# Recurrence levels on TensorE taken two at a time, with copies of half of q, in a two-layer hybrid model on one core

## The chip, the cores and the metric

The kernel runs on one core of a Trainium2 chip, in float32. The metric is the device time of one execution in microseconds, the median of several runs. [...] Each engine runs its own list of instructions in order and waits on semaphores for the others.

## What is computed

Two layers over a sequence of 256 tokens and 1024 features. Each layer is: feed-forward, a mixer, cross-attention over 256 memory rows, feed-forward, each with a residual and a layer norm. The change is inside the mixer, in the gated linear recurrence (four heads, 128 by 128 state). From the reference, cut:

```python
f = lb + (1.0 - lb) * jax.nn.sigmoid(f_logit)      # decay, per token and feature
k = 1.0 - f
def step(state, inp):                              # one chunk of tokens
    b = jnp.cumsum(lb_, axis=2)                    # lb_: log f
    decay = exp(b[t] - b[s]) for s <= t, else 0
    attn = einsum('bhtd,bhsd,bhtsd->bhts', qb, kb, decay)
    o = attn @ vb + (qb * exp(b)) @ state
    ...
o = o * rsqrt(mean(o**2) + RMS_EPS) * norm_g * sigmoid(g)
```

Beside the recurrence the mixer has a gated short convolution and a pooling over windows of 2, 4, 8 and 16 tokens; the three results are joined and multiplied by `w_out`.

## The kernel before, in words

All large products are made with weights split in a high and a low half: ScalarE casts the high half (`whi`, L61), VectorE subtracts to get the low half (`wlo`, L62), and TensorE adds three products (hi x hi, hi x lo, lo x hi; `product`, L105). Raw weights come by SP's DMAs into six buffers (`raw`, L77); a buffer is free for the next load when both halves have been made from it. There are eight buffers each for `whi` and `wlo`.

`mixer` (L779) makes, from one weight matrix `w_in`, the decay `f` and `k = 1 - f`, then `q`, and after that, piece by piece, the values `v` (in four half-products), the pooling input `pu` (two), the convolution's `cv` (four) and `u` (two). These twelve pieces are a generator, `between` (L855); `products_of_others(n)` (L863) takes the next n of them. So the big products are spread between the steps of the recurrence, on TensorE in the order in which the code is written (`manual_schedule`, L867). On the other engines a scheduler orders the instructions, except in the short VectorE part at L1008.

The recurrence isn't computed token by token. The decay between two tokens is a product of `f` over the tokens between them, and it is built over seven levels of block size c = 1, 2, 4, ..., 64 (`LEVELS`). At level c, tokens in the later block of each pair of blocks attend to those in the earlier block. `k` and `q` carry the decay up to the edge of their block:

- `q` is first multiplied by `f` in place (L892); before that, the squares (L888) multiply `k` and `q` of the same block of 32 tokens, and the diagonal is kept by a mask (L889).
- `blocks(c)` (L896) copies the earlier blocks of `k` to a dense tile `kc` on ScalarE (L899), with two buffers.
- At L923, 16 matmuls of 128x32 weights (four groups of PSUM partitions by four heads) multiply `kc` and the later blocks of `q`, which are read in place with a stride.
- VectorE then multiplies half of `k` (L935) and half of `q` (L938) by the block products `tot`, in place, for the next level. The product with `q` has to wait until TensorE has read `q` at this level.
- What a level gives is kept from PSUM: below 32 by a masked copy into `square` (L947), from 32 on by ScalarE into `AT` (L960); `square` itself goes to `AT` at L957.

In the profile each of these float32 matmuls appears as two records: the squares as 64, a level as 32. Between two levels stand one or two pieces of the other products.

After the last level come the product of the first half's `k` with the second half's `q` (L971, copied to `AX_`, L972), the recurrence's two products with `v` (L981, L982), its norm (`ss`: squares on ScalarE L986, a power on POOL L988), and the gate's four products. `yr` (L995) is dealt by small DMAs (L1002) and transposed back (L1058). The pooling sums go through two tiles `pw` in turn (L1024, L1030), end in `win` (L1032) and are multiplied on TensorE (L1047), between the gate's last product and the four products for the attention's keys (`fill`, L1061). `project_back` then multiplies by `w_out` in slabs of two row blocks, in the order 0, 6, 2, 4.

Of the kernel before, what the change touches and what calls it, by code (L numbers as in the profile page):

```python
# [8 lines left out]
F32 = mybir.dt.float32  # L9
# [3 lines left out]
ALU = mybir.AluOpType  # L13
# [4 lines left out]
P = 128  # L18
DEPTH = 2
SEQ = 256  # L20
DM = 1024
DFF = 2816
NT = SEQ // P
NK = DM // P
HEADS = 4
# [4 lines left out]
LEVELS = (1, 2, 4, 8, 16, 32, 64)  # L30
WINDOWS = (2, 4, 8, 16)
PAD = 16
# [14 lines left out]
def model(ctx: ExitStack, tc: tile.TileContext, t: dict, out: bass.AP):  # L47
    nc = tc.nc
# [5 lines left out]
    def acc(shape=(P, 2, SEQ), tag="acc"):  # L54
        return ps.tile(list(shape), F32, tag=tag, name=tag)
# [88 lines left out]
    h = [cst.tile([P, DM], F32, name=f"h{i}") for i in range(NT)]  # L144
# [69 lines left out]
    idc = consts[:, 0:32]  # L214
# [564 lines left out]
    def mixer(l, fill):  # L779
        w_in = t["w_in"][l]  # L780
        with tc.tile_pool(name="mix", bufs=1, reuse_waits="tile") as mp:
# [81 lines left out]
            def products_of_others(n):  # L863
                for _ in range(n):
                    next(fill_in)
# [18 lines left out]
            o = acc((P, NT, HEADS, 32), "dn")  # L884
            for b in range(NT):
                for hh in range(HEADS):
                    for g in groups:
                        nc.tensor.matmul(o[g, b, hh, :], k[:, b, hh, g], q[:, b, hh, g], start=True, stop=True)  # L888
            nc.vector.tensor_tensor(  # L889
                square, o, idc[:, None, None, :].to_broadcast([P, NT, HEADS, 32]), op=ALU.mult  # L890
            )
            nc.vector.tensor_tensor(q, q, f, op=ALU.mult)  # L892
            qf, kf = q[:, :, :, :], k[:, :, :, :]
            tot = f.rearrange("p b h s -> p (b h s)")

            def blocks(c):  # L896

                kc = mp.tile([P, HEADS, P], F32, tag="kc", name="kc", bufs=2)
                nc.scalar.copy(  # L899
                    kc.rearrange("p h (a w c) -> p w (h a) c", w=2, c=c),  # L900
                    view(kf, 0, (other + c, 2), (2 * c, HEADS * 64 // c), (1, c), keep=True),
                )
                return kc

            def later(j, c):

                at = (j * 32 // c ^ 1) * c
                return slice(at, at + c)

            kc = blocks(1)  # L910
            for n, c in enumerate(LEVELS):
                a = 64 // c
                products_of_others((1, 2, 1, 2, 1, 2, 2)[n])


                o = acc((P, HEADS, max(c, 32)), "dn")
                for hh in range(HEADS):
                    for j, g in enumerate(groups):
                        if c < 32:
                            x = view(qf, hh * P + 32 * j + c, (other - c, 2), (2 * c, 16 // c), (1, c))  # L920
                        else:
                            x = q[:, j * 32 // c % 2, hh, later(j, c)]
                        nc.tensor.matmul(o[g, hh, :], kc[:, hh, g], x, start=True, stop=True)  # L923
                na, tb = HEADS * a, other // c
                q2 = view(qf, c, (other - c, 2), (2 * c, na), (1, c))
                k2 = view(kf, 0, (other + c, 2), (2 * c, na), (1, c))
                tq = bass.AP(
                    tensor=tot.tensor, offset=tot.offset,
                    ap=[list(tot.ap[0]), [tb + 1, 2], [2, na]] + ([[0, c]] if c > 1 else []),
                )  # L930
# [4 lines left out]
                nc.vector.tensor_tensor(k2, k2, tk, op=ALU.mult)  # L935
                if c < 64:
                    kc = blocks(2 * c)
                nc.vector.tensor_tensor(q2, q2, tq, op=ALU.mult)  # L938
                if c < 64:
                    nt = mp.tile([P, NT * na], F32, name=f"tot{c}")  # L940
                    t2 = tot.rearrange("p (a w) -> p a w", w=2)
                    nc.vector.tensor_tensor(nt, t2[:, :, 0], t2[:, :, 1], op=ALU.mult)
                    tot = nt[:, :]
                if c < 32:
                    o = o.rearrange("p h (b t) -> p h b t", b=NT)
                    for b in range(NT):
                        nc.vector.copy_predicated(  # L947
                            square[:, b].rearrange("p h (a w c) -> p h a w c", w=2, c=c)[:, :, :, 1 - b, :],
                            masks[:, b, n, :].rearrange("p (a c) -> p a c", c=c)[:, None].to_broadcast(
                                [P, HEADS, 16 // c, c]  # L950
                            ),
                            o[:, :, b].rearrange("p h (a c) -> p h a c", c=c),
                        )
                else:
                    if c == 32:
                        for g in groups:
                            nc.scalar.copy(AT[g, :, :, g], square[g])  # L957
                    for at in range(0, P, c):
                        g = slice(at, at + c)
                        nc.scalar.copy(AT[g, at // c % 2, :, later(at // 32, c)], o[g])  # L960
            w_gate = load(w_in, 0, NK, 2304, 512)

            def gate(j, o=None):
# [257 lines left out]
```

## Time and profile before

| | before |
|---|---|
| median of 3 runs | 1070.83 us (1070.54 to 1071.65) |
| span of the profiled execution | 1068.8 us |
| mean granted TensorE clock | 0.998 |
| VectorE, ScalarE busy | 946.3 us, 642.4 us |
| one mixer's recurrence, first layer | 212.5 to 255.3 us from the span's start |
| the same, second layer | 738.8 to 781.6 us |

The span goes from the first to the last instruction of one profiled execution; it has no time of its own beside the span, and the runs' median is 2.0 us longer. In a row of the timeline the numbers are the start, how long the group took, the engine, the line and operation, out <- in, the shape and the count; a note in brackets tells of idle time before it and what ended it. PE is TensorE's matmul, PEld its weight load. L numbers are lines of the kernel above.

### The profile page before, as it was taken

Reading aid. Unit: us, or ns where it says so; the run is one execution under the profiler, and the core shown is the slowest. Engines: PE = TensorE matmul, PEld = TensorE weight load, DVE = VectorE, ACT = ScalarE, POOL = GpSimd, SP = SyncE. Lnnn points to the kernel's source line nnn. Section 1 sums busy time; section 2 is a strip of 40 time slices with the busy share of each in tenths; the row PEclk is TensorE's granted clock in tenths of the full one; section 3 lists DMA queues with packets and bytes.
Section 4 is the critical chain, followed back from the end, with each engine's and each line's share of the span. In section 5 each row is a group of like instructions: output and inputs, shape, how many; then the busy total and the mean of one; then the engine's idle time right before and its main releaser. Section 6 shows DMA issues by size and latency. Waiting matters only on the chain.

```text
span 1068.8 us, 16312 instructions
## 1 busy us (share of the span) xinstructions
PE 1059.3 (99%) x5966; PEld 937.7 (88%) x5966; DVE 946.3 (89%) x1318; ACT 642.4 (60%) x916; POOL 66.4 (6%) x114
## 2 busy tenths in 40 slices
PE   9999999999999999999999999999999999999997
PEld 7888888889899888888888888888898998888886
DVE  6977997998988799999799999788989787999996
ACT  7555664666557565656575557566764665656660
POOL 9700001000000000000000000010000000000000
PEclk9999999999999999999999999999999999999999
DMA  9997484755574575848675865856536665759461
GB/s 362 262 307 256 129 288 165 249 176 174 170 278 167 178 252 194 290 167 218 238 272 184 256 254 183 290 179 216 196 126 213 241 227 181 257 156 334 134 223 40
DMA packets 130895, 231.90 MB, mean 217 GB/s; under 512 B 9408, under 2 KB 48608, under 8 KB 130816
## 3 DMA queue, kind: packets, MB, share of 16 engines
q1 hardware_dynamic: 129024, 228.49, 64.8%
q0 software_dynamic: 1216, 1.20, 0.5%
q8 instruction: 47, 0.77, 0.3%
q10 hardware_dynamic: 576, 1.18, 0.3%
q14 instruction: 32, 0.26, 0.1%
HBM read 216.15 MB, written 1.05 MB: 203 GB/s over the span
## 4 chain that ended last, share of the span: by engine, by line
PE 99%; DMA 0%; DVE 0%; issue 0%; DVEq 0%
PE acc L105 65%; PE dn L105 31%; PE acc L172 1%; PE dn L923 1%; PE dn L982 0%; DMA h<-in_x_dram 0%; PE acc L491 0%; PE dn L981 0%; PE dn L971 0%; PE acc L1047 0%; PE dn L888 0%; DVE h L358 0%; DVE h L353 0%; PE dn L472 0%; DVE st L338 0%
## 5 line engine op out<-in xcount | busy, mean ns | idle before, releaser
L61 ACT CAST whi<-raw 128x1024 fp32r<-128x1024 f32 (+1 forms) x438 | 442.9, 1042 | 197.5 <-DVE raw L597 54.9
L62 DVE TENSOR_TENSOR wlo<-raw,whi 128x1024 fp32r<-128x1024 f32 (+1 forms) x438 | 515.7, 1209 | 32.6 <-ACT whi L61 29.0
L105 PE MATMUL acc<-whi,xT 128*128 128x512 f32 x1032 | 312.9, 380 | 0.0
L105 PEld LDWEIGHTS acc<-whi,xT 128*128 128x128 f32 x1032 | 195.1, 189 | 27.5
L105 PE MATMUL acc<-wlo,xT 128*128 128x512 f32 x516 | 195.6, 379 | 0.0
L105 PE MATMUL acc<-xT,whi 128*128 128x512 f32 x576 | 142.3, 383 | 0.2
L105 PE MATMUL dn<-whi,ah 128*128 128x512 f32 x346 | 131.5, 380 | 0.0
L105 PE MATMUL dn<-wlo,ah 128*128 128x512 f32 x346 | 131.2, 379 | 0.0
L105 PE MATMUL dn<-whi,al 128*128 128x512 f32 x346 | 131.2, 379 | 0.0
L105 PEld LDWEIGHTS acc<-xT,whi 128*128 128x128 f32 x576 | 104.0, 190 | 12.5 <-ACT whi L61 0.7
L105 PEld LDWEIGHTS acc<-wlo,xT 128*128 128x128 f32 x516 | 97.5, 189 | 13.8
L105 PE MATMUL dn<-whi,xT 128*128 128x512 f32 x288 | 87.9, 381 | 0.0
L105 PEld LDWEIGHTS acc<-xT,wlo 128*128 128x128 f32 x576 | 75.5, 191 | 3.9
L105 PE MATMUL acc<-xT,wlo 128*128 128x256 f32 x576 | 75.9, 275 | 0.0
L105 PEld LDWEIGHTS dn<-whi,al 128*128 128x128 f32 x346 | 65.4, 189 | 9.2
L105 PEld LDWEIGHTS dn<-wlo,ah 128*128 128x128 f32 x346 | 65.4, 189 | 9.2
L105 PEld LDWEIGHTS dn<-whi,ah 128*128 128x128 f32 x346 | 65.4, 189 | 9.1
L350 POOL TENSOR_TENSOR rs<-rs,nhalf 128x1 f32<-128x1 f32 x16 | 14.9, 930 | 833.6 <-DVE rs L346 598.1
L597 DVE TENSOR_TENSOR raw<-raw 128x1024 f32<-128x1024 f32 x56 | 66.2, 1217 | 0.4
L105 PEld LDWEIGHTS dn<-whi,xT 128*128 128x128 f32 x288 | 54.4, 189 | 7.7 <-DVE xT L62 0.3
L105 PE MATMUL dn<-wlo,xT 128*128 128x512 f32 x144 | 54.6, 379 | 0.0
L332 DVE SCALAR_TENSOR_TENSOR h<-h,dn 128x512 f32<-128x512 f32 x31 | 21.2, 683 | 32.9 <-PE dn L105 32.9
(234 smaller groups left out, 1277.5 us busy)
## 6 DMA issues: line engine op xcount, KB each, us to landing
raw<-in_ffn_up_dram SPq DMA_DIRECT2D x88, 512.0 KB, 5.3
raw<-in_ffn_down_dram SPq DMA_DIRECT2D x88, 512.0 KB, 6.6
raw<-in_ffn_gate_dram SPq DMA_DIRECT2D x84, 512.0 KB, 5.1
raw<-in_w_in_dram SPq DMA_DIRECT2D x48, 512.0 KB, 4.7
dealt<-sg SPq DMA_DIRECT2D x80, 128.0 KB, 4.7
raw<-in_ca_k_dram SPq DMA_DIRECT2D x16, 512.0 KB, 4.9
raw<-in_w_out_dram SPq DMA_DIRECT2D x16, 512.0 KB, 4.5
raw<-in_ca_v_dram SPq DMA_DIRECT2D x16, 512.0 KB, 5.3
```

The lines of the kernel that those rows point to most:

```text
L61: nc.scalar.copy(hi, src)
L62: lows.append(nc.vector.tensor_tensor(lo, src, hi.bitcast(F32), op=ALU.subtract))
L105: nc.tensor.matmul(o, w, x, start=start, stop=stop)
L172: nc.tensor.transpose(pt[:, k, :], src[:, (4 * j + k) * P : (4 * j + k + 1) * P], unit)
L332: nc.vector.scalar_tensor_tensor(v, v, ALPHA / scale, sums(y[i][n]), op0=ALU.mult, op1=ALU.add, accum_out=None if junk is None else st[:, ...
L350: nc.gpsimd.tensor_tensor(rs, rs, nhalf[:, 0:1], op=ALU.pow)
L597: nc.vector.tensor_tensor(r[i], r[i], plus[i], op=ALU.add)
L923: nc.tensor.matmul(o[g, hh, :], kc[:, hh, g], x, start=True, stop=True)
```

## The change

- Order on TensorE: the squares and level 1 stand directly behind one another, then levels 2 and 4, 8 and 16, 32 and 64, with three pieces of the other products ahead of each of the last three pairs. Before, each level had one or two pieces ahead of it.
- `q * f` goes to a new tile `q1` (the squares still read `q`), and the levels work on `q1`.
- For levels 2, 8 and 32, ScalarE copies the later halves of `q1` to a dense tile `qc`, and the matmuls of that level read `qc`. VectorE's product with `q1` at these levels waits for that copy in place of the level's matmuls.
- `kc` is made for both levels of a pair ahead of it (the same two buffers).
- `qc` and `AX_` no longer have tiles of their own: `qc` lives in the first `pw` tile's place and `AX_` in the second's. The `pw` tiles are made, and their pads cleared by POOL, after the recurrence.

```diff
-            AX_ = mp.tile([P, HEADS, P], F32, name="AX_")
...
-            pw = [mp.tile([P, 2, PAD + SEQ], F32, name=f"pw{n}") for n in range(2)]
-            for x in (pu, *pw):
-                nc.gpsimd.memset(x[:, :, 0:PAD], 0.0)
+            nc.gpsimd.memset(pu[:, :, 0:PAD], 0.0)
+
+            def window(n, name):
+                return mp.tile([P, 2, PAD + SEQ], F32, tag=f"pw{n}", name=name)
+
+            def in_window(n, name):
+                return window(n, name).rearrange("p a t -> p (a t)")[:, 0:512]
...
-            nc.vector.tensor_tensor(q, q, f, op=ALU.mult)
-            qf, kf = q[:, :, :, :], k[:, :, :, :]
+            q1 = mp.tile([P, NT, HEADS, P], F32, name="q1")
+            nc.vector.tensor_tensor(q1, q, f, op=ALU.mult)
+            qf, kf = q1[:, :, :, :], k[:, :, :, :]
...
-            def blocks(c):
+            def earlier_of_k(c):
...
+            def later_of_q(c):
+
+                qc = in_window(0, "qc").rearrange("p (b t) -> p b t", b=NT)
+                nc.scalar.copy(
+                    qc.rearrange("p b (a c) -> p b a c", c=c),
+                    view(qf, c, (other - c, 2), (2 * c, HEADS * 64 // c), (1, c), keep=True),
+                )
+                return qc
...
-            kc = blocks(1)
-            for n, c in enumerate(LEVELS):
-                a = 64 // c
-                products_of_others((1, 2, 1, 2, 1, 2, 2)[n])
...
+            kc = earlier_of_k(1)
+            products_of_others(1)
+            o = acc((P, NT, HEADS, 32), "dn")
+            for b in range(NT):
+                for hh in range(HEADS):
+                    for g in groups:
+                        nc.tensor.matmul(o[g, b, hh, :], k[:, b, hh, g], q[:, b, hh, g], start=True, stop=True)
+            o1 = attention_within(1, kc)
+            of_k(1)
+            kc = earlier_of_k(2)
+            nc.vector.tensor_tensor(
+                square, o, idc[:, None, None, :].to_broadcast([P, NT, HEADS, 32]), op=ALU.mult
+            )
+            of_q(1)
+            kept(0, 1, o1)
+            for n, c in ((1, 2), (3, 8), (5, 32)):
+                qc = later_of_q(c)
+                of_k(c)
+                kd = earlier_of_k(2 * c)
+                of_q(c)
+                products_of_others(3)
+                o = attention_within(c, kc, qc)
+                o2 = attention_within(2 * c, kd)
+                of_k(2 * c)
+                if c < 32:
+                    kc = earlier_of_k(4 * c)
+                of_q(2 * c)
+                kept(n, c, o)
+                kept(n + 1, 2 * c, o2)
+                if c == 8:
+                    for g in groups:
+                        nc.scalar.copy(AT[g, :, :, g], square[g])
+            products_of_others(1)
...
-                nc.tensor.matmul(o[:, hh, :], k[:, 0, hh, :], q[:, 1, hh, :], start=True, stop=True)
+                nc.tensor.matmul(o[:, hh, :], k[:, 0, hh, :], q1[:, 1, hh, :], start=True, stop=True)
+            AX_ = in_window(1, "AX_").rearrange("p (h t) -> p h t", h=HEADS)
             nc.scalar.copy(AX_, o)
...
+            pw = [window(n, f"pw{n}") for n in range(2)]
+            for x in pw:
+                nc.gpsimd.memset(x[:, :, 0:PAD], 0.0)
```

The functions `of_k`, `of_q`, `attention_within` and `kept` hold what the loop over the levels held: the product of half of `k`, the product of half of `q` with the next `tot`, the 16 matmuls, and what keeps a level's result. `attention_within(c, kc, qc)` reads `qc` where one is given and `q1` otherwise.

More of the change, by code (lines that the diff above doesn't have):

```diff
@@ L883, in mixer @@
             groups = [slice(32 * j, 32 * j + 32) for j in range(4)]
[L884 to L891, printed above, removed]
-            nc.vector.tensor_tensor(q, q, f, op=ALU.mult)
-            qf, kf = q[:, :, :, :], k[:, :, :, :]
-            tot = f.rearrange("p b h s -> p (b h s)")
-            def blocks(c):
+            q1 = mp.tile([P, NT, HEADS, P], F32, name="q1")
+            nc.vector.tensor_tensor(q1, q, f, op=ALU.mult)
+            qf, kf = q1[:, :, :, :], k[:, :, :, :]
+            tots = [f.rearrange("p b h s -> p (b h s)")]
+            def earlier_of_k(c):
                 kc = mp.tile([P, HEADS, P], F32, tag="kc", name="kc", bufs=2)
@@ L908, in later, with of_k @@
                 return slice(at, at + c)
-            kc = blocks(1)
-            for n, c in enumerate(LEVELS):
+            def of_k(c):
                 a = 64 // c
-                products_of_others((1, 2, 1, 2, 1, 2, 2)[n])
[L916 to L923, printed above, removed]
                 na, tb = HEADS * a, other // c
-                q2 = view(qf, c, (other - c, 2), (2 * c, na), (1, c))
+                tot = tots[-1]
                 k2 = view(kf, 0, (other + c, 2), (2 * c, na), (1, c))
[L927 to L930, printed above, removed]
                 tk = bass.AP(
@@ L935, in mixer, with of_q @@
                 nc.vector.tensor_tensor(k2, k2, tk, op=ALU.mult)
-                if c < 64:
-                    kc = blocks(2 * c)
+            def of_q(c):
+                a = 64 // c
+                na, tb = HEADS * a, other // c
+                tot = tots[-1]
+                q2 = view(qf, c, (other - c, 2), (2 * c, na), (1, c))
+                tq = bass.AP(
+                    tensor=tot.tensor, offset=tot.offset,
+                    ap=[list(tot.ap[0]), [tb + 1, 2], [2, na]] + ([[0, c]] if c > 1 else []),
+                )
                 nc.vector.tensor_tensor(q2, q2, tq, op=ALU.mult)
@@ L942, in mixer, with attention_within, kept @@
                     nc.vector.tensor_tensor(nt, t2[:, :, 0], t2[:, :, 1], op=ALU.mult)
-                    tot = nt[:, :]
+                    tots.append(nt[:, :])
+            def attention_within(c, kc, qc=None):
+                o = acc((P, HEADS, max(c, 32)), "dn")
+                for hh in range(HEADS):
+                    for j, g in enumerate(groups):
+                        if c < 32:
+                            if qc is None:
+                                x = view(qf, hh * P + 32 * j + c, (other - c, 2), (2 * c, 16 // c), (1, c))
+                            else:
+                                x = qc[:, :, hh * 64 + j * 16 : hh * 64 + j * 16 + 16]
+                        elif qc is None:
+                            x = q1[:, j * 32 // c % 2, hh, later(j, c)]
+                        else:
+                            x = qc[:, j % 2, hh * 64 + j // 2 * 32 : hh * 64 + j // 2 * 32 + 32]
+                        nc.tensor.matmul(o[g, hh, :], kc[:, hh, g], x, start=True, stop=True)
+                return o
+            def kept(n, c, o):
                 if c < 32:
```

6 lines of the change are left out of this document (3 added, 3 removed).

## The prediction

> **What bounds the kernel now.** I read the page first (busy times and the chain that ended last), then who waited for whom on TensorE, then the chain in order of time around one mixer, then the timeline of single instructions there. Two lines of the page, and TensorE's whole list of waits:
>
> ```profile
> span 1068.8 us, 16312 instructions
> PE 1059.3 (99%) x5966; PEld 937.7 (88%) x5966; DVE 946.3 (89%) x1318; ACT 642.4 (60%) x916; POOL 66.4 (6%) x114
> ```
>
> ```profile
> PE dn L472 <- DVE kTh L467: 1.5, 1, 1.5
> PE acc L491 <- DMA h<-in_x_dram: 0.5, 1, 0.5
> ```
>
> TensorE is busy for 99% of the span and waited twice, both at the very start. No other engine is on the path for more than the edges, so time can be won only by giving TensorE less to do, and is lost only by making it wait. VectorE, at 89%, is the engine that could make it wait.
>
> The recurrence of a mixer puts eight short runs of 128x32 matmuls between long runs of 128x128 ones. The timeline shows what each of them costs beyond its own matmuls:
>
> ```profile
> 212.14 0.38 PE L105 MATMUL acc<-whi,xT 128*128 128x512 f32 x1
> 212.45 0.76 PE L888 MATMUL dn<-q,k 128*32 128x32 f32 x64
> 213.47 0.38 PE L105 MATMUL acc<-wlo,xT 128*128 128x512 f32 x1
> ```
>
> ```profile
> 224.59 0.38 PE L105 MATMUL acc<-xT,whi 128*128 128x512 f32 x1
> 224.91 0.46 PE L923 MATMUL dn<-q,kc 128*32 128x32 f32 x32
> 225.29 1.78 PE L105 MATMUL acc<-xT,whi 128*128 128x512 f32 x7
> 226.91 1.05 PE L105 MATMUL acc<-xT,wlo 128*128 128x256 f32 x8
> 227.80 1.89 PE L105 MATMUL acc<-xT,whi 128*128 128x512 f32 x8
> 229.53 1.05 PE L105 MATMUL acc<-xT,wlo 128*128 128x256 f32 x8
> ...
> 233.94 0.46 PE L923 MATMUL dn<-q,kc 128*32 128x32 f32 x32
> ...
> 245.59 0.66 PE L923 MATMUL dn<-q,kc 128*32 128x64 f32 x32
> ```
>
> Undisturbed, eight 512-column matmuls go from start to start in 229.53 - 227.80 = 1.73 us, 0.216 each. Around the level at 224.91 the same eight (one before it, seven behind) take 226.91 - 224.59 = 2.32 us. So a run of 32 small records costs 0.59 us. The run of the squares, L888, has 64 records: 213.47 - 212.14 = 1.33 us for two large matmuls that need 0.43, so it costs 0.90. Twice the records cost 0.31 more, not 0.59 more: **0.28 us of every run is the price of breaking into the large matmuls and returning to them**, and 0.31 is the work. The rows show it on both sides: 0.32 us from the last large matmul's start to the first small one, where 0.22 is usual, and seven large ones in 1.62 us behind it, where 1.51 is usual.
>
> **The change, part by part.**
>
> *Fewer runs on TensorE.* In the order of the changed program as built, the squares and level 1 stand in one run of 96 records, then 2 with 4, 8 with 16 and 32 with 64: four runs per mixer in place of eight. No matmul is added, dropped or resized. Four breaks less in each of two mixers: 8 x 0.28 = 2.24 us. The merged runs aren't in the trace; L888 is the nearest row to them. From both sides: if records in the middle of a run go at the 0.27 us for 32 that the first ones of a run take (0.59 less 0.32), a break is worth 0.32 and the sum 2.5; the lower end follows.
>
> *A wait inside a run.* Level 1, 4, 16 and 64 now follow another small run at once and wait for two engines each; the first wait is an instruction of its own in the queue.
>
> ```profile
> L923 PEld LDWEIGHTS dn<-q,kc x448: 105/113/117, 215.9 to 772.3; 128*32 128x32 f32 x150
> L923 PEldq EVENT_SEMAPHORE  x14: 51/51/51, 215.6 to 769.2; - x14
> ```
>
> ```profile
> 216.00 0.39 PE dn L923 x31
> ...
> 239.83 0.39 PE dn L923 x32
> ...
> 771.96 0.58 PE dn L923 x32
> ```
>
> It takes 51 ns. In the kernel before it ran while large matmuls were still busy: the last one starts at 769.2 and its run at 771.96, a lead of 2.7 us. Inside a run of small records (0.31 us for 32) the lead is shorter, and no row shows such a wait there. Bounds: 0 if the queue still holds 51 ns of work, 8 x 51 ns = 0.41 us if it doesn't. I take 0, since the runs with it (L923) begin as soon after the last large matmul as L888, which has none (0.32 and 0.31 us), and keep 0.41 for the range: the sum is then -1.83. [...]
>
> *The moving operand.* Levels 2, 8 and 32 read q from a dense copy. In the chain's rows above, level 1 with its stride of two (216.00) and level 32, dense already (239.83), both have 0.39 us, so I take nothing, and nothing to lose.
>
> *Three more copies on ScalarE, per mixer.* They have the form of L899 (first row):
>
> ```profile
> L899 ACT COPY kc<-k 128x512 f32<-128x512 f32 x14 | 9.6, 683 | 13.3 <-DVE k L935 11.2 <-DVE k L810 2.1
> L935 DVE TENSOR_TENSOR k<-k,tot 128x512 f32<-128x512 f32 x12 | 8.6, 717 | 1.9 <-ACT kc L899 1.9
> ```
>
> ```profile
> 218.70 2.94 ACT L61 CAST whi<-raw 128x1024 fp32r<-128x1024 f32 x3
> ```
>
> 3 x 0.68 = 2.0 us on an engine that is busy for 60%. They lie in the chain k product (the last row), copy, q copy, q product (0.7 like the k product) that must end before a pair. I walked the new order with these durations and, from start to start, 0.95 us for a cast of weights on ScalarE (three in 2.94) and 1.14 for VectorE's half (four in 4.63, a row below). The pairs' last input is ready at 220.1, 229.2 and 237.5; TensorE reaches them at 224.0, 232.8 and 241.5 (the old starts 224.91, 233.94, 245.59, less the runs, breaks and the one product that no longer stand ahead). Some 4 us are spare at each. The first run is closer: scaled q is ready at 214.0, and its level comes at 215.7. If this cover went, each us late would cost one us.
>
> *q's new home* is the same multiplication into another tile: no cost. It is moved ahead of the squares, which then wait for TensorE alone.
>
> *The window sums go late.* `pw` now shares its two homes with the copy of q and with `AX_`. So `pw1` can be written only after the recurrence's second product, and POOL's clearing of its pad stands behind the first `ss` power. VectorE's busy time by stretch, and what is late next:
>
> ```profile
> 212.00:232.00 20.00, 20.00 (x283) 16.82 (x282) 19.00 (x32) 11.53 (x18) 0.00 (x0) 1.00 0.68 228
> 232.00:249.00 17.00, 17.00 (x191) 15.02 (x190) 15.65 (x35) 12.52 (x25) 0.00 (x0) 1.00 0.51 166
> 249.00:259.70 10.70, 10.70 (x77) 10.09 (x76) 6.58 (x20) 6.63 (x23) 2.03 (x2) 1.00 0.35 115
> 259.70:278.90 19.20, 19.20 (x109) 17.33 (x108) 19.20 (x29) 13.63 (x21) 0.00 (x0) 1.00 0.49 160
> ```
>
> ```profile
> L1024 DVE TENSOR_TENSOR pw<-pw x6: 409/426/677, 231.2 to 760.9; 128x256 f32<-128x256 f32 x4, 128x512 f32<-128x512 f32 x2
> L1024 DVE TENSOR_TENSOR pw<-pu x2: 693/693/693, 229.4 to 755.8; 128x512 f32<-128x512 f32 x2
> ```
>
> ```profile
> 237.10 0.69 DVE L1032 TENSOR_TENSOR win<-win,pu 128x512 f32<-128x512 f32 x1
> ```
>
> ```profile
> L986 ACT ACTIVATE square<-dn 128x128 f32<-128x128 f32 x16 | 4.4, 277 | 1.5 <-PE dn L982 1.1
> ```
>
> ```profile
> 276.60 4.63 DVE L62 TENSOR_TENSOR wlo<-raw,whi 128x1024 fp32r<-128x1024 f32 x4
> ```
>
> ```profile
> 254.87 0.39 PE L982 MATMUL dn<-v,AT 128*128 128x128 f32 x2
> 260.33 1.03 PE L1047 MATMUL acc<-win,wpool 128*128 128x256 f32 x4
> 280.31 0.38 PE L105 MATMUL dn<-wlo,xT 128*128 128x512 f32 x1
> ```
>
> In the stretches the third busy figure is VectorE's: full at 259.7 to 278.9, with 10.70 - 6.58 = 4.1 us free just before. A mixer's window steps (four passes, four small pieces, the subtraction) are 0.69 + 0.68 + 2 x 0.42 + 0.69 + 4 x 0.17 = 3.6 us by their durations and 2.9 in a row, where neighbours overlap by 0.08 as the weight halves do. In the new order only the first pass and piece come before 249; 2.2 us fall into that free time.
>
> The walk: the second product ends at 254.87 + 0.39 - 1.12 = 254.1. Then VectorE does `pw1`, the gate's scaling, the first `yr` and a piece (0.6, 0.5, 0.6 and 0.1: 255.9); `ss` waits for ScalarE's four squares (0.4 each with the read of the sum) and a window pass between them, 256.2; two passes, two pieces, ScalarE's last pass and the subtraction follow (0.3, 0.1, 0.3, 0.1, 0.5, 0.6): 258.2. TensorE asks for `win` at 260.33 - 1.12 = 259.2: 1.0 us spare, where 22 were (237.8 to 260.33). From 258.2 on VectorE has a gate's adds and the second `yr`, 1.0 us, which stood just ahead of 259.7, and then the work of the full stretch, 19.2 us, in another order (one half of w_out's weights now behind the transposes): w_out's last half is made at 278.4. Before, as the second of the four at 276.60, it was made at 278.9. TensorE's first use was at 280.31 and is now at 279.2: 0.8 us spare. SP issues the last w_out load when the late half frees its buffer, near 269 in place of 262; 4.5 us to landing (the median of w_out's loads, below) and a cast end well before VectorE's turn. I cost all this at nothing, with the 1.0 and 0.8 us as the cover that a longer walk would use up. POOL's queue: its next work, the second `ss` power, comes 2 us later than the clearing, so nothing is held.
>
> ```profile
> raw<-in_w_out_dram SPq DMA_DIRECT2D x16, 512.0 KB, 4.5
> ```
>
> **Sum.** -2.24 us on the path of the span of 1068.8 us, which becomes 1066.6. The median of the runs is 1070.83; 2.0 us lie around the span, and nothing in them is touched. Forecast: 1068.6 us, 0.21% less. A difference of 0.2%, 2.1 us, is about what a measurement of this kernel can tell from no change, so the forecast lies at that line.
>
> **The rivals.**
>
> *The wait inside the run shows* (-1.83 us, and down to -1.4 where each pause costs twice its length): 1069.0 to 1069.4, no difference. For it: records follow each other every 8 to 10 ns there. Against it: the lead of 2.7 us.
>
> *The late window work is partly in TensorE's way.* Where VectorE is 0.8 to 2.7 us later than walked, w_out's last half makes TensorE wait by what exceeds 0.8, in each mixer: 1068.6 + 2 x (0 to 1.9), so up to 1072.4. The stretch at 259.7 is full, and my walk has some 30 steps; but the free 4.1 us ahead of it are real.
>
> *Slower: the window work isn't absorbed.* VectorE's free time at 249 to 259.7 is waiting in order for ScalarE and TensorE. If the 2.2 us of window steps don't fit into it and the pass that waits for the second product holds back gate and `yr` by another us, the full stretch ends 3.2 us later than walked. TensorE then waits 3.2 - 0.8 = 2.4 us per mixer against 1.12 saved: +2.6 us, 1073.4. It decides from 3.0 us of lateness on (2 x (3.0 - 0.8 - 1.12) = 2.1). For it: w_out's halves are the only weights without a stretch of spare time ahead of them. Against it: of the 4.1 us, 2 are left by my walk.
>
> *It doesn't do what it says*: the order as built has the four runs, so this could only be a break that stays inside a run, which is the first rival.
>
> **How the numbers follow.** The forecast (-1.9 to -2.6) gets 0.60, five in six of it beyond 0.2%; the exposed wait 0.12; the partial stall 0.11, nearly all within 0.2% either way; the slower case 0.17. Faster 0.50, same 0.10 + 0.12 + 0.11 = 0.33, slower 0.17. The range goes from 1067.9 (-2.5 us and 0.4 for the runs' spread) to 1071.0, which takes in the exposed wait and the smaller stalls and leaves out the slower case and little more.
>
> **What would show it.** In the profile after: four runs per mixer in the chain, of about 96, 64, 64 and 64 records, the large blocks around them with 0.2 us over their undisturbed time once per run; a pair of 32s at 0.9 us in all. A pair near 0.95 to 1.0 is the exposed wait. A row that TensorE waited for VectorE at the pooling product or at w_out's last half is the late window work; its size is the loss. A wait of a pair's first level for ScalarE would mean that the copies lie on the path, which I exclude by 4 us.

## The result, and the profile after

The changed kernel takes 1068.80 us (median of 21 runs, 1068.28 to 1070.98) against 1070.83 for the kernel before (21 runs, 1070.44 to 1071.71): a ratio of 0.9981, 95% interval 0.9975 to 0.9987. That is 2.03 us less, where 2.2 were forecast. The profiled execution has a span of 1067.8 us where 1068.8 stood before, only 1.0 less; experiment 5 takes up the difference.

The page of the kernel after, and TensorE's waits (us in total, times, longest). In these rows DVE is VectorE, ACT is ScalarE, POOL is GpSimd, and SP is SyncE, whose queue issues all 396 loads of `raw`:

```profile
PE 1057.5 (99%) x5966; PEld 938.0 (88%) x5966; DVE 946.6 (89%) x1318; ACT 646.6 (61%) x922; POOL 66.9 (6%) x114
```

```profile
PE dn L472 <- DVE kTh L467: 1.5, 1, 1.5
PE acc L105 <- DVE wlo L62: 0.8, 1, 0.8
PE acc L491 <- DMA h<-in_x_dram: 0.5, 1, 0.5
```

TensorE has the same 5966 records and is busy for 1.8 us less. The second row is new. Its place is 600 us, in a feed-forward block and far from the mixer.

The timeline of the kernel after shows the runs of the first mixer:

```profile
214.80 0.38 PE L105 MATMUL acc<-whi,xT 128*128 128x512 f32 x1
215.11 0.76 PE L980 MATMUL dn<-q,k 128*32 128x32 f32 x64
215.86 0.46 PE L955 MATMUL dn<-q,kc 128*32 128x32 f32 x32
...
216.56 0.38 PE L105 MATMUL acc<-wlo,xT 128*128 128x512 f32 x1
...
223.93 0.38 PE L105 MATMUL acc<-xT,whi 128*128 128x512 f32 x1
224.24 0.46 PE L955 MATMUL dn<-qc,kc 128*32 128x32 f32 x32
224.52 0.49 PE L955 MATMUL dn<-q,kc 128*32 128x32 f32 x32
224.94 1.78 PE L105 MATMUL acc<-xT,whi 128*128 128x512 f32 x7
226.55 1.05 PE L105 MATMUL acc<-xT,wlo 128*128 128x256 f32 x8
```

There are four runs per mixer, as the program says. From the last large start ahead of the pair to the first start of eight behind it go 226.55 - 223.93 = 2.62 us; eight undisturbed ones need 1.73, so the pair costs 0.89 us. That is the price of the 64 records of the squares before (0.90), and 0.28 less than two single levels (2 x 0.59). The first run costs 216.56 - 214.80 - 0.43 = 1.33 us.

Counted run by run in the trace, the small runs cost 5.20 us per mixer before (0.89 + 6 x 0.59 + 0.78). After, they cost 1.33 + 0.89 + 0.89 + 1.08 = 4.19 in the first mixer and 4.08 in the second, whose first run took 1.22. Together that is 2.13 us less.

The late work on VectorE, and where TensorE first needs it (timeline of the kernel after):

```profile
258.00 0.69 DVE L1082 TENSOR_TENSOR win<-win,pu 128x512 f32<-128x512 f32 x1 [0.26 <-ACT win L1080]
...
259.40 1.03 PE L1097 MATMUL acc<-win,wpool 128*128 128x256 f32 x4
...
276.69 4.66 DVE L62 TENSOR_TENSOR wlo<-raw,whi 128x1024 fp32r<-128x1024 f32 x4
...
279.38 0.38 PE L105 MATMUL dn<-wlo,xT 128*128 128x512 f32 x1
```

`win` ends at 258.7 (before the change at 237.8) and is needed at 259.4: 0.7 us spare. The second of the four halves ends at 276.69 + 4.66 / 2 = 279.0 and is needed at 279.38: 0.4 us spare. TensorE waits at neither.

### The profile page after: what moved, and what is told of

It reads as the page before. It is cut to its first block, busy times and chain, and to the rows that moved or that the text cites. A ratio compares the mean times of both kernels' runs of the same rounds, so it can differ in the third digit from the quotient of the medians.

```text
span 1067.8 us, 16332 instructions
## 1 busy us (share of the span) xinstructions
PE 1057.5 (99%) x5966; PEld 938.0 (88%) x5966; DVE 946.6 (89%) x1318; ACT 646.6 (61%) x922; POOL 66.9 (6%) x114
## 3 DMA queue, kind: packets, MB, share of 16 engines
q10 hardware_dynamic: 576, 1.18, 0.3%
## 4 chain that ended last, share of the span: by engine, by line
PE 92%; DVE 5%; issue 1%; DMA 1%; ACT 1%; SPq 0%; DVEq 0%; ACTq 0%
PE acc L105 60%; PE dn L105 30%; DVE wlo L62 2%; PE acc L172 1%; DVE raw L597 1%; DMA dealt<-sg 1%; PE dn L955 0%; ACT whi L61 0%; DMA h<-in_x_dram 0%; PE dn L1029 0%; DVE h L358 0%; DVE sg L440 0%; PE acc L491 0%; DVE square L453 0%; DVE h L353 0%
```

## The experiments

**1. The breaks alone: eight_runs and by_heads.** eight_runs keeps every edit but puts the large products back between the levels:

```diff
-                products_of_others(3)
+                products_of_others(2)
                 o = attention_within(c, kc, qc)
+                products_of_others(2 if c == 32 else 1)
                 o2 = attention_within(2 * c, kd)
```

and the same between the squares and level 1.

> The changed kernel with its eight runs of small matmuls apart again, with large products between them as before the change; q1, the copies of q, the shared homes and the late window sums stay. Theory (a break costs 0.28 us and nothing else of the change has a price): eight breaks more, +2.24 us, 1071.0, the time of the kernel before (1070.8). Rival (the rest of the change gains or costs by itself): the time then lies off the time of the kernel before by that amount, say 1071.5 or more if the late window sums cost, and 1070.3 or less if the copies gain. Rival (the fewer breaks are not the cause): it stays at 1068.8.

Measured: 1070.99 us (11 runs), ratio 0.9999 (0.9990 to 1.0008). So the merged runs are the whole gain. Scaled `q`'s new tile, the copies and the late window sums have together no price that can be measured; in the trace each mixer takes as long as before, within 0.01 us.

by_heads goes the other way. Between the large matmuls of one product, each pair is issued in eight pieces:

```diff
+                for hh in range(HEADS):
+                    pieces.append(lambda hh=hh: attention_within(c, kc, qc, o, [hh]))
+                for hh in range(HEADS):
+                    pieces.append(lambda hh=hh: attention_within(2 * c, kd, None, o2, [hh]))
+                products_of_others(1)
```

> The changed kernel, but each pair's 64 records are issued as eight pieces of 8 records (one head each), one piece behind each of the first large matmuls of the product that stood ahead of the pair. Same matmuls, 7 breaks more per pair, 42 in all. Theory (each break has a fixed price of 0.28 us, however short the run): +11.8 us, 1080.6. Rival (the price is one of filling and emptying a queue, which a piece of 8 records with one large matmul around it doesn't pay in full): half of it or less, +5.9 us, 1074.7. Rival (a piece also loses the overlap of its own records): above 1081.

Measured: 1082.29 us (4 runs), 13.5 more than the changed kernel, or 0.32 per break where the theory had 0.28. Its timeline:

```profile
222.36 0.27 PE L962 MATMUL dn<-qc,kc 128*32 128x32 f32 x8
222.56 0.48 PE L105 MATMUL acc<-xT,whi 128*128 128x512 f32 x1
222.97 0.27 PE L962 MATMUL dn<-qc,kc 128*32 128x32 f32 x8
```

One period, 222.97 - 222.36 = 0.61 us, holds one large matmul (0.216) and eight records (0.08). What is left, 0.31 to 0.32, is the break, and the period repeats as long as large matmuls of 512 columns stand between. The time lies in the range of the second rival (above 1081), but not for its reason: the eight records of a piece start within 0.073 us, as the first eight of a whole run do. So the price doesn't fall with the length of the run, and it is 0.32 rather than 0.28. Merging two runs of 32 wins only 0.28, because the second 32 records of a run go a little slower: start to start the first 32 take 0.27 us and the next 0.30 (trace of the changed kernel, pair at 224.24).

**2. What a break is made of: whole_array.** The levels below 64 use the whole array, without another shape. Only one of four groups of 32 rows of each product is kept, so this version leaves the levels' results out:

```diff
-                        nc.tensor.matmul(o[g, hh, :], kc[:, hh, g], x, start=True, stop=True)
+                        if whole:
+                            nc.tensor.matmul(wide[:, j, hh, :], kc[:, hh, :], x, start=True, stop=True)
...
```

> The changed kernel, but levels 1 to 32 use the whole array: 128x128 weights (a head's whole kc) and the same 32 moving columns, as many matmuls as before, and of the products only one of four groups of 32 rows is kept, so the levels' results are left out. The squares and level 64 keep their 128x32 shape. Theory (the price of a break is that of changing the array's shape): the runs of levels 2 with 4 and 8 with 16 show no gap at their ends, 0.22 us or less from the last large matmul to the first small one and 0.22 from the first large one behind to the next, where the changed kernel has 0.31 and 0.32. Rival (the price is that of going from long to short matmuls): 0.31 and 0.32 stay. The records themselves get longer: the whole-array matmuls of 128 columns start every 0.112 us, a quarter of that is 0.028 per record in place of 0.009, so 12 levels x 32 x 0.019 = +7.3 us, less about 1.2 for four breaks by the theory: 1075; more if short records have a floor above 0.028.

Measured: 1130.19 us (4 runs), far over the 1075. In its timeline are the entry of a whole-array run in the first mixer, the exit of one in the second, and there the step from whole-array records (L961) to those of level 64, which keep the 128x32 shape (L963):

```profile
230.60 0.38 PE L105 MATMUL acc<-xT,whi 128*128 128x512 f32 x1
230.82 1.42 PE L961 MATMUL dn<-qc,kc 128*128 128x32 f32 x12
...
776.05 1.06 PE L961 MATMUL dn<-q,kc 128*128 128x32 f32 x8
776.94 0.46 PE L105 MATMUL acc<-whi,xT 128*128 128x512 f32 x1
777.24 0.38 PE L105 MATMUL acc<-wlo,xT 128*128 128x512 f32 x1
...
827.97 0.39 PE L961 MATMUL dn<-qc,kc 128*128 128x32 f32 x2
828.29 0.26 PE L963 MATMUL dn<-q,kc 128*32 128x64 f32 x4
```

At the entry the usual 0.22 us stand where a 128x32 run has 0.31. At the exit the first large start comes 0.112 us behind the last small one, a record's own length, where a 128x32 run has 0.126 against 0.009 per record; then 0.30 to the next, where it has 0.32. So the 0.09 at the entry goes with the change of shape. The step into level 64 shows it a second time, with short records on both sides: 828.29 comes 0.205 us behind the last L961 start (828.08), 0.09 more than the 0.112 between such records.

The 0.12 at the exit can't be given to the shape by these rows. The whole-array records of this run come 0.112 us behind one another, and where the squares go over into whole-array records of level 1, the first comes 0.125 behind. So by these rows the change of shape adds some 0.01 to the exit, and the rest may be the 0.112 that lie between whole-array records in any case; no run separates the two. Of the last 0.10, 0.08 stays without a change of shape (0.30 where 0.22 is usual). What TensorE does in the 0.09 us at the entry, no row here shows.

The expected time was wrong because a record on the whole array takes 0.112 us with 32 columns (L961 here) as with 128 (L971 of the kernel before), not 0.028. What sets that pace isn't shown: the weight-load records of this run last 186 to 192 ns at the full clock, longer than the 0.112 us from one record to the next, and overlap. Then the granted clock fell as well (stretch of the long run, and a part of it; PEclk is the third figure from the end):

```profile
230.00:241.00 11.00, 11.00 (x75) 10.79 (x75) 3.67 (x9) 1.74 (x4) 0.00 (x0) 0.76 0.37 136
236.00:239.00 3.00, 3.00 (x16) 3.00 (x16) 0.00 (x0) 0.00 (x0) 0.00 (x0) 0.50 0.00 0
```

The 0.76 is a mean: the clock stood at 1.00 and then at 0.50. In the pairs of levels 2 to 16 the fall came between the 34th and the 45th record, after 3.6 to 4.8 us of them, and from there one took 0.213 us. Small tiles are worth their break here.

**3. The cover of the late window work: late_more, late_second, early_windows.** late_more makes the first window pass four times (`for _ in range(1 if g else 4)`), late_second the second pass five times. early_windows gives the sums tiles of their own again:

```diff
-                qc = in_window(0, "qc").rearrange("p (b t) -> p b t", b=NT)
+                qc = q[:, 0].rearrange("p h s -> p (h s)").rearrange("p (b t) -> p b t", b=NT)
...
-            AX_ = in_window(1, "AX_").rearrange("p (h t) -> p h t", h=HEADS)
+            AX_ = mp.tile([P, HEADS, P], F32, tag="kc", name="AX_", bufs=2)
```

> The changed kernel with the first pass of the window sums made four times over (the same sums into the same tile): three passes more on VectorE per mixer, 3 x 0.61 to 0.69 = 1.8 to 2.1 us, in the late place. Theory (VectorE has about 0.4 us to spare at the last half of w_out's weights and 0.7 at the subtraction that ends win): TensorE waits 1.4 to 1.7 us per mixer, +2.8 to +3.4 us, 1071.6 to 1072.2. Rival (VectorE's waits in this stretch take it in): 0 to +0.8 us, 1068.8 to 1069.6, with no wait of TensorE at either place.

> The changed kernel with the second pass of the window sums, the first that has to wait for the recurrence's second product, made five times over: four passes more on VectorE per mixer, 4 x 0.61 = 2.44 us, all of it in the late place. Theory (VectorE has 0.7 us to spare at win, 0.4 at w_out's last half and some 0.5 of waiting in order on the way): TensorE waits some 1.2 us for win and 0.3 more for w_out's last half in each mixer, +3.0 us, 1071.8, between 1071.0 and 1072.9 (nothing taken in on the way). Rival (the stretch takes it in, as it took in most of the three passes made earlier): under 1069.6 and no wait at win.

> The changed kernel with tiles of their own for the window sums again, so that they may run as early as before the change; the copies of q's halves go into q's tile, which is free behind the squares, and AX_ into one of kc's two homes. Runs of small matmuls as in the changed kernel. Theory (the late sums cost nothing): 1068.8, within 0.4 us. Rival (they hold TensorE up for a few tenths in some executions): 1068.0 to 1068.4 and no first use of w_out's last half close behind VectorE.

late_more: 1069.78 us (11 runs; 0.9978 to 0.9996 of before), 1.0 over the changed kernel, where 2.8 to 3.4 had been expected. The first pass needs only `pu`: in the first mixer all four were made by 249.4 us, ahead of the late place, and VectorE was only some 0.35 us late by the end (its last four halves start at 277.03 in place of 276.69, while TensorE was 0.2 us ahead of its place in the changed kernel). The timeline of late_more shows that as a wait, 0.67 us where 0.43 are usual for two:

```profile
278.76 0.59 PE L105 MATMUL dn<-whi,xT 128*128 128x512 f32 x2
279.43 0.48 PE L105 MATMUL dn<-wlo,xT 128*128 128x512 f32 x1
```

So the cover at w_out's last half is some 0.3 us. Each mixer of this profile won 0.74 to 0.77 us where the changed kernel's win 1.13 to 1.15 (experiment 5); that is 0.75 of the 1.0. late_second: 1076.07 us (5 runs), 7.3 over the changed kernel for 2 x 2.44 us of work. TensorE's waits there:

```profile
PE dn L105 <- DVE wlo L62: 3.4, 2, 1.7
...
PE dn L105 <- DVE xT L62: 1.0, 2, 0.5
PE dn L105 <- ACT xT L61: 0.8, 2, 0.4
```

```profile
267.42 0.48 PE L105 MATMUL dn<-wlo,xT 128*128 128x512 f32 x1 [1.71 <-DVE wlo L62]
...
268.17 1.03 PE L1098 MATMUL acc<-win,wpool 128*128 128x256 f32 x4
```

The loss is larger than the work added, and I had expected 3.0. The scheduler gave TensorE another order here: first products with `w_out` stand ahead of the one with `win` (268.17, in the changed kernel 259.40), and TensorE waited for their inputs three times, 2.6 us in each mixer. `win` itself ended only at 268.0. How much of the loss is the new order and how much the late inputs isn't separated. early_windows: 1068.80 us (11 runs; 0.9972 to 0.9990), the same as the changed kernel. The lateness that the change brings costs nothing; the added passes of late_more and late_second, 2 us and more per mixer, do cost.

**4. The copies: copies_four.** Each copy of `q` is made four times over (`for _ in range(4)` around it).

> The changed kernel with each of ScalarE's three copies of q's halves per mixer made four times over: 3 x 0.68 = 2.0 us more on ScalarE ahead of each pair. Theory (some 4 us are spare at each pair, and ScalarE is busy for 60%): no wait of TensorE at the pairs, 1068.8 within 0.5 us. Rival (the copies lie near the path): TensorE waits at the pairs' first level, up to 3 x 2 x 2.0 us; half of that would be 1075.

Measured: 1072.00 us (11 runs), 3.2 over the changed kernel; I had expected nothing. TensorE's waits:

```profile
PE acc L1098 <- DVE win L1083: 0.8, 1, 0.8
PE acc L1098 <- PE acc L105: 0.8, 1, 0.8
...
PE dn L956 <- DVE q L936: 0.2, 1, 0.2
```

and the timeline of ScalarE and VectorE ahead of the first pair:

```profile
222.16 1.15 ACT L61 CAST whi<-raw 128x1024 fp32r<-128x1024 f32 x1
223.11 0.92 ACT L905 COPY qc<-q 128x512 f32<-128x512 f32 x1
...
224.48 0.72 DVE L936 TENSOR_TENSOR q<-q,tot 128x512 f32<-128x512 f32 x1
```

The scheduler put two casts of weights between the copies, so 2.0 us more of copies made `q` some 5 us later (225.2; in the changed kernel 219.8). The 4 us of cover were there and were used up: the first pair costs 1.12 us in the first mixer and 1.25 in the second, where the changed kernel has 0.89. Most of the loss comes later. Against its place in the changed kernel TensorE falls back by some 1.0 us at `win` (the first two rows are this wait, one in each mixer) and 0.4 at w_out's last half in each mixer; by which steps the copies make these late wasn't followed. One copy per pair is free; the cover isn't to be spent in ScalarE's microseconds alone.

**5. The wait inside a run: level_first.** Level 1 stands ahead of the squares, so that no wait is left inside the first run.

```diff
+            o1 = attention_within(1, kc)
             o = acc((P, NT, HEADS, 32), "dn")
...
-            o1 = attention_within(1, kc)
```

> The changed kernel with level 1 ahead of the squares in the first run. The squares' inputs are the older ones, so no wait stands inside this run any more. Theory (the wait behind 64 records cost 0.01 us in most executions and up to 0.14 in one): the first run costs 1.19 us beyond its large matmuls in both mixers, with no instruction of the queue inside it; time 1068.7, not to be told from the changed kernel. Rival (the late second part of the run has another cause, such as the supply of instructions): a pause behind the 64th record stays, with no wait there.

Measured: 1069.14 us (11 runs; 0.9974 to 0.9992), not to be told from the changed kernel. The first run costs 1.18 us in both mixers, with no pause. For comparison, the changed kernel profiled again:

> The changed kernel, unaltered, profiled once more. Theory (the 0.75 us that TensorE waited for VectorE at 600 us, and the 0.13 us more at level 1 in the first run, belong to one execution and not to the change): neither comes back; span 1067.8 less 1.0, about 1066.8 to 1067.0, and a first run of 1.20 us beyond its large matmuls. Rival (they belong to the changed order): both are there again, span 1067.8.

Span 1067.2 us, of which 0.53 is a later start of the whole (at 174 us, ahead of the mixer, TensorE is 0.61 behind the kernel before, in the first profile 0.08). Each mixer won 1.13 to 1.15 us, and at 600 us nothing was lost. Its first run:

```profile
215.34 0.38 PE L105 MATMUL acc<-whi,xT 128*128 128x512 f32 x1
...
216.26 0.46 PE L955 MATMUL dn<-q,kc 128*32 128x32 f32 x32
...
216.97 0.38 PE L105 MATMUL acc<-wlo,xT 128*128 128x512 f32 x1
```

1.20 us, so the wait behind 64 records costs 0.02. The 1.33 in the first profile is not a thing of that execution alone: the first mixers of copies_four and late_second have 1.32 and 1.30, those of four other versions with this run 1.20. In the three long ones the wait's instruction ran 0.60 to 0.64 us into the run in place of 0.50, though scaled `q` was ready 0.94 us before the run in all of them; the cause stays open. For the 0.75 us at 600 (by TensorE's place 1.02 us are lost there) the transfers tell more. In the first profile and in the second (553 to 564 us; KB each, median us from issue to landing):

```profile
raw<-in_ffn_down_dram SPq DMA_DIRECT2D x2, 512.0 KB, 5.7
raw<-in_ffn_gate_dram SPq DMA_DIRECT2D x2, 512.0 KB, 6.8
dealt<-sg SPq DMA_DIRECT2D x4, 128.0 KB, 6.5
```

```profile
raw<-in_ffn_down_dram SPq DMA_DIRECT2D x2, 512.0 KB, 4.3
raw<-in_ffn_gate_dram SPq DMA_DIRECT2D x2, 512.0 KB, 5.4
...
dealt<-sg SPq DMA_DIRECT2D x4, 128.0 KB, 4.3
```

Where they land 1.4 to 2.2 us later, ScalarE's and VectorE's halves don't follow the earlier TensorE, and it runs into them. three_runs, below, has the same wait in its profile and the slowest transfers there (6.0, 7.2 and 6.9 us); level_first, with 5.6, 6.2 and 5.7, loses 0.2 us. That slower transfers come with the stall is shown; what makes them slow in one execution and not in another isn't.

**6. Fewer runs still: two_runs and three_runs.** two_runs puts levels 2 to 64 in one run of 192 records; the copies live in `q`'s and `AT`'s tiles and in those of the layer norm's parameters, which are loaded later:

```diff
+            for c in LEVELS[1:6]:
+                made[c] = earlier_of_k(c), later_of_q(c)
+                of_k(c)
+                of_q(c)
+            products_of_others(9)
+            small = acc((P, 4, HEADS, 32), "dn")
+            os = [attention_within(c, *made[c], small[:, n]) for n, c in enumerate(LEVELS[1:5])]
+            os.append(attention_within(32, *made[32]))
+            os.append(attention_within(64, None))
```

> A version with two runs of small matmuls per mixer: the squares with level 1, and levels 2, 4, 8, 16, 32 and 64 together, 192 records in one run at the place of the changed kernel's last pair. It needs ten homes for the copies: kc's two, q's tile, AT's tile (cleared behind the run) and the two tiles of the layer norm's parameters, which are loaded later; the window sums have tiles of their own, as in early_windows. Level 64 reads k itself. Theory (0.28 us per break, waits inside a run hidden): four breaks fewer than the changed kernel, -1.13 us, 1067.7. Rival (a wait inside a run is hidden only at its beginning, while the queue still holds work from ahead of the run; the sequencer loses its lead within some 60 records): four of the five waits cost 0.05 to 0.13 us each, in two mixers +0.4 to +1.0, 1068.1 to 1068.7. Rival (the results of six levels at once come too late for the recurrence's second stage): a wait of TensorE at AT's first use, above 1068.8.

> The version with two runs, unaltered, profiled once more. Theory (the 3.2 us for which the long run of the second mixer stood still with nothing to wait for come from the supply of instructions, whose blocks end at a fixed place of the program): it stands still again near the same record of the second mixer, for 1 to 4 us. Rival (it was an event of one execution): no pause over 0.1 us in either long run. The 1.6 us of waiting behind the long run should be there in at least one mixer in either case, since the eviction of six levels is part of the order.

Measured: 1073.30 us (9 runs; 1.0013 to 1.0032 of before), slower than both kernels. In the first mixer the long run cost 2.17 us, 0.69 less than the three pairs (0.89 + 0.89 + 1.08), with no instruction of the queue inside it. But then TensorE waited 1.6 us (1.3 in two_again) for VectorE, which was keeping six levels. In the second mixer the run stood still inside level 64, in both profiles behind its fifth record. TensorE's waits and the timeline of two_again:

```profile
PE dn L962 <- issue: 2.6, 1, 2.6
...
PE acc L105 <- DVE square L969: 1.3, 1, 1.3
```

```profile
767.34 0.30 PE L962 MATMUL dn<-q,k 128*32 128x64 f32 x4
770.26 1.06 PE L962 MATMUL dn<-q,k 128*32 128x64 f32 x27 [2.63 <-issue]
771.25 2.77 PE L105 MATMUL acc<-xT,whi 128*128 128x512 f32 x7
773.86 1.05 PE L105 MATMUL acc<-xT,wlo 128*128 128x256 f32 x8
```

The profile names no engine that was being waited for. The clock fell as well: about the end of the pause the granted clock went from 1.00 to 0.50 for 3.4 us in both profiles, and the next seven large matmuls took 773.86 - 771.25 = 2.61 us in place of 1.62. Pause and clock together lose some 4 us, more than the merged runs of both mixers save. The transfers of that half microsecond (two_again, 767.5 to 768.0) hold a load of instructions:

```profile
q8 instruction: 1, 0.02, 11.5%
```

It lies at 767.8, 0.4 us behind the beginning of the pause; in the first profile at 768.9, 0.5 behind it. In the first mixer, where the run doesn't pause, the load comes at 243.7, 1.8 us behind the run. So the pause goes with a load of instructions, as the theory for two_again had it; whose instructions they are the row doesn't say, and that the supply makes the pause is argued and not shown. Of the rivals for two_runs, that of exposed waits fell, and that of results kept too late stands, at 1.3 to 1.6 us in the first mixer; neither foresaw the pause.

three_runs merges less: level 1 with the squares, then 2, 4, 8, then 16, 32, 64.

```diff
+            for n, levels, products in ((1, (2, 4, 8), 4), (4, (16, 32, 64), 5)):
...
+                products_of_others(products)
+                os = [attention_within(*x) for x in made]
```

> A version with three runs of small matmuls per mixer: level 1 with the squares (level 1 first), levels 2, 4 and 8 behind the sixth of the products that lie between, levels 16, 32 and 64 at the place of the changed kernel's last pair. The copies live in kc's two homes, q's tile and the two tiles of the layer norm's parameters, which are loaded later; the window sums have tiles of their own. Theory (0.28 us per break, waits in a run of 96 records hidden or below 0.05 us): two breaks fewer than early_windows (1068.8), -0.56 us, 1068.2; the two longer runs at 0.90 + 0.30 = 1.20 and 1.39 us in place of 0.89 + 0.89 + 1.08. Rival (the results of three levels at once hold up VectorE and ScalarE, as six did in two_runs): TensorE waits behind a run for a bank to come free, 0.5 us or more per mixer, 1069.3 or more.

Measured: 1068.21 us (11 runs), ratio 0.9979 (0.9970 to 0.9988): the fastest median here, but its interval overlaps the changed kernel's. By the trace it wins what was expected: its long runs cost 1.20 and 1.37 us in the first mixer, and with the first run's 1.19 that makes 3.76 where after_again has 4.06. Its spans have a median of 1066.1 us, 1.0 less than the changed kernel's 1067.1, but each run takes 2.1 us beyond its span where the changed kernel's take 1.7; why isn't known.

## Why the prediction was right, point by point

- *The price of a break.* Right in sum, mis-sized as a thing. Forecast -2.24 us; the runs of after_again give 2 x (5.20 - 4.06) = 2.28, and the first profile 2.13. The 0.28 was taken as the price of leaving and returning. by_heads shows 0.32 for that; in a merged run 0.04 of it goes back, because the records of its second half are slower. For merging runs of 32, and for taking them apart again (eight_runs: 2.19 us for eight breaks), the difference of two rows was the right number; for the short pieces of by_heads it was 12% low.
- *The wait inside a run.* Taken as nothing; in the pairs it is nothing (0.89 = 0.89), in the first run 0.02 us in most profiles and up to 0.14 in three (experiment 5). The source view of the changed kernel has the instruction:

```profile
L955 PEldq EVENT_SEMAPHORE  x8: 51/51/51, 215.7 to 768.0; - x8
```

  Behind 32 records it ran 0.10 to 0.14 us into the run, 0.13 to 0.17 ahead of the record that it holds up; behind 64, in after_again and most others, at 0.50 us of 0.57. At 0.0084 us a record (0.27 for 32) and 0.0094 (0.30 for 32) the queue is ahead by some 18 records at the first place and by about 7 at the second, an estimate from these times. The prediction took the wait to be hidden; that holds for the pairs, and the lead shrinks along a run. How much work the queue can hold, no run shows.
- *The moving operand, q's new home.* Nothing, as forecast: eight_runs has both and the time of the kernel before.
- *The copies.* Hidden, as forecast; the pairs' last inputs were walked to 220.1, 229.2 and 237.5 and came at 220.3, 228.4 and 237.6, some 4 us ahead of TensorE as said. But "each us late would cost one us" left out that the order on ScalarE changes with the load (experiment 4).
- *The window sums.* Walked: `win` 258.2, last half 278.4, with 1.0 and 0.8 us spare. Measured: 258.7 and 279.0, with 0.7 and 0.4. The walk was 0.5 to 0.6 us early in 30 steps (its last steps, as printed, add up to 258.1), and the verdict held because the spare time was larger than that error. With 0.3 to 0.4 us left that was near. late_more shows the rival's place to be the right one: beyond some 0.3 us w_out's last half is where TensorE waits.
- *Span against median.* The sum gave a span of 1066.6; the profiled one was 1067.8, mostly because of the wait outside the mixer, where 1.02 us are lost and which the second profile doesn't have. The runs, at -2.03 us, are nearer to the sum than the one profile is. The "2.0 us around the span" compared a median with the span of another execution: each run of either kernel takes 1.7 us more than its own span, and the profile before was 0.3 faster than its median. The forecast doesn't suffer, since it takes the difference from the median.

## What to carry to other kernels

When small matmuls of another tile shape stand between large ones, price the run and the break separately, by two runs of different length, and then join runs before anything else is tuned. Join only as far as the engines that clear the results can follow: two levels at a time won (1068.80 us against 1070.83), three won by the trace (spans 1.0 us shorter again), six lost (1073.30 us, with 1.3 to 1.6 us of waiting for VectorE in the first mixer, beside the pause in the second). Where a step moves onto an engine that is full, its spare time is what lies between its end and its first use in the profile; a tenth of a microsecond is worth counting there, and a change of load changes the scheduler's order too.

## What the runs showed of the hardware that was not expected

- A break into 128x32 matmuls costs 0.32 us (by_heads, 0.61 us per period). At the entry 0.09 of it goes with the change of the array's shape (0.31 us where 0.22 is usual); whole-array runs of float32 matmuls enter in the usual 0.22 us (whole_array), and their exit costs 0.08 beyond the records' own 0.112.
- In whole_array a 128x128 float32 record takes 0.112 us with 32 moving columns as with 128, and in runs of 64 such records the granted clock fell from 1.00 to 0.50 after 3.6 to 4.8 us.
- In a run of 192 small records TensorE stood still for 2.8 to 3.2 us at the same record in two profiles (two_runs, two_again), from 0.4 to 0.5 us ahead of a load of instructions on, and the granted clock then was 0.50 for 3.4 us.
- One execution's transfers landed 1.4 to 2.2 us later than another's over 11 us, and that was enough to give back the gain of a mixer: a single profile of a kernel whose engine is 99% busy can be 0.7 us off the median of its runs' spans, about a third of the gain measured here.
